# Encoder block on one core: sums of row blocks made in the merging stage and kept in DRAM, and a new start of the up-projection

## The chip, the cores and the metric

The kernel runs as one launch on one core of one Trainium2 chip. Times are device microseconds of that core, from the first to the last instruction of an execution. Its engines are TensorE (PE, with its weight loads PEld), VectorE (DVE), ScalarE (ACT), GpSimd (POOL) and SyncE (SP, which only issues DMAs).

## The reference

One encoder block over 2048 tokens of 1024 channels, in float32. What matters here is its end:

```
merged = sigmoid(g_a) * br_a + sigmoid(g_b) * br_b      # attention branch, conv branch
x  = x + merged @ w_out
h2 = rmsnorm(x, norm2_g)
up = dwconv3(h2 @ w_up)                # w_up: 1024 x 5632
gate, val = split(up, 2)
x  = x + (gelu(gate) * val) @ w_down   # w_down: 2816 x 1024
out = rmsnorm(x, norm_f_g)
```

## The kernel before

Every float32 operand of a matmul is split into a high part (ACT copies it, rounded, line 88) and a low part (DVE subtracts, line 89), and a product is three matmuls: high by high, high by low, low by high.

The program has three stages. The first makes the input projection, attention and convolution; the change leaves it alone. The second, the merging stage (`phase_b`), goes over four quads of 512 tokens. A quad has 8 blocks of `merged`, then four token tiles of 128 tokens with 48 matmuls of `w_out` each (line 835). Behind a token tile, DVE adds the residual (L844) and SP stores it; ACT sums the squares (L125), POOL works out the inverse root in eight tiny steps (L119, L105, then L108 and L109 three times) and DVE scales the rows (L850). `h2_tiles` then transposes two such tiles, chunk by chunk of 128 channels, on PE (L872); ACT copies them out times the norm's gain (L875) and SP stores them to the DRAM tensor `h2` (L877). These steps lie between matmuls of later tiles. The last two tiles have none to lie between.

The third stage is the feed-forward. Tokens are halved: `phase_up(0)`, `phase_down(0)`, `phase_up(1)`, `phase_down(1..3)`. `phase_up` multiplies by `w_up` in 22 pairs of row blocks, a gate block and a value block of 128 channels, by a form with seven products instead of eight. With A the weights (two blocks of channels by two halves of K) and B the activations (two halves of K by two blocks of 512 tokens), the products are A11·B11, A12·B21, S1·T1, S2·T2, S3·T3, S4·B22 and A22·T4. S1 to S4 are sums of weight blocks, T1 to T4 sums of activation blocks. Each product is 12 matmuls of 128x512 (four chunks `kc` of K, three each, line 951), 84 for a pair.

At the start of each `phase_up`, `h_raw` loads two blocks of 512 KB from `h2` for each `kc` (L894), POOL makes T1 to T4 out of them (L905, four of 128x512), and ACT and DVE split the seven tiles `h`. The split tiles stay, 28 of them, for all 22 pairs. `w_raws` loads two blocks of 512 KB of weights for a pair (L923), POOL makes four sums (L934 to L937), and seven tiles `w` are split. For the first pair, `head` issues three of the products `kc` by `kc`, so that they can run while the tiles arrive; from then on `unit` takes product after product.

PE's instructions stand in the order of the code, which in the merging stage interleaves transposes by a period in matmuls. The other engines' orders come from the program's builder. Each queue is in order: an instruction that waits holds those behind it. SP issues nearly all DMAs.

Of the kernel before, what the change touches and what calls it, by code (L numbers as in the profile page):

```python
# [12 lines left out]
F32 = mybir.dt.float32  # L13
# [42 lines left out]
PAD_ACT = 256  # L56
F_RAW, F_W, F_U, F_C, F_BLK = 4, 9, 3, 2, 4
# [4 lines left out]
TAGS_B = {"gt": "gt", "x": "x", "lv": "lv", "h2": "h2", "y": "y"} | {n: "l" for n in _LN}  # L62
BUFS_B = {"gt": 2, "x": 4, "l": 6, "lv": 1, "h2": 4, "y": 1}
# [14 lines left out]
class Block:  # L78
# [651 lines left out]
    def phase_b(self):  # L730
        nc, a = self.nc, self.a
        mm = nc.tensor.matmul
# [81 lines left out]
        def main():  # L814
# [5 lines left out]
            for qd in range(4):  # L820
# [6 lines left out]
                for tt in range(4):  # L827
# [23 lines left out]
                    xs.append(y)  # L851
# [4 lines left out]
                self.sides.append([self.h2_tiles(xs[2:4], t0 - 128), 2.4, -4.0])  # L856
# [6 lines left out]
    def h2_tiles(self, xs, t0):  # L863

        n = 2
        st = None
        for kc in range(KC):
            if kc % n == 0:
                st = self.T([128, n, 256], name="h2")
            ps = self.pp.tile([128, 512], F32, name="pt", tag="s")  # L870
            for i, x in enumerate(xs):
                self.nc.tensor.transpose(  # L872
                    ps[:, i * 128 : i * 128 + 128], x[:, kc * 128 : kc * 128 + 128], self.ident
                )
            self.nc.scalar.activation(st[:, kc % n], ps[:, :256], AF.Copy, scale=self.col(C_G2, kc))  # L875
            if kc % n == n - 1:
                self.nc.sync.dma_start(  # L877
                    self.h2[kc - n + 1 : kc + 1, :, t0 : t0 + 256].rearrange("k p t -> p k t"), st
                )
            yield  # L880
# [8 lines left out]
    def h_raw(self, half, kc):  # L889
        t0 = half * HALF  # L890
        out = []
        for k in (kc, kc + 4):
            r = self.k4("hraw", "raw", F_RAW)
            self.nc.sync.dma_start(r, self.h2[k, :, t0 : t0 + HALF])  # L894
            out.append(r)
        return out
# [62 lines left out]
    def phase_up(self, half):  # L959
# [41 lines left out]
        def unit(f, W, tail, u):  # L1001
# [6 lines left out]
            if tail:  # L1008
                tail()
# [208 lines left out]
```

## Time and profile before

| | us |
|---|---|
| median of 3 runs | 2851.57 (2850.73 to 2852.62) |
| the profiled execution | 2845.32 |
| its span | 2843.5 |
| PE busy | 2729.9 (96%) |
| DVE, ACT, POOL busy | 1939.1, 1184.8, 543.7 |
| mean granted TensorE clock | 0.979 |

The page cuts the span into 40 slices of 71 us. The merging stage fills slices 16 to 20, `phase_up(0)` begins in slice 21 at about 1435 us and `phase_up(1)` in slice 29 at about 2016 us. Two rows of the slices stand in the section on rows, below. Busy time of matmuls is modelled and a few per cent of matmul records can be missing, so a count (x46) may be a little low.

### The profile page before, as it was taken

The numbers are of one execution on the slowest core, as the hardware profiler recorded it, in microseconds if no ns is written. First come the engines' busy times: TensorE is split into PE (matmuls) and PEld (weight loads), VectorE is DVE, ScalarE is ACT, GpSimd is POOL, SyncE is SP. The second block draws the span as 40 slices with busy tenths as digits, with TensorE's granted clock in tenths as the row PEclk, the third lists the DMA queues.
The fourth block names the chain that finished last, engine by engine and source line by source line (L and its number), as shares of the span: only waits on it lengthen the run. The fifth ranks groups of instructions, "written<-read, shape, count | busy, mean of one in ns | idle before, by whom it ended". The sixth has DMA issues, their size and how long they took to land.

```text
span 2843.5 us, 34321 instructions
## 1 busy us (share of the span) xinstructions
PE 2729.9 (96%) x12597; PEld 2254.7 (79%) x12597; DVE 1939.1 (68%) x2636; ACT 1184.8 (42%) x1880; POOL 543.7 (19%) x698
## 2 busy tenths in 40 slices
PE   8998999999999999999959999999799999999998
PEld 6786788888888878888838888888588888888877
DVE  4697999677876746665368888883588888834342
ACT  6422222256655633332245455452354554533231
POOL 1101000000000001001054444421544344102021
PEclk9999999999999999999969999999899999999999
DMA  5357733589788777766342222254222222555451
GB/s 176 96 155 238 249 120 118 159 219 256 208 241 221 208 244 237 245 208 208 100 138 89 85 89 75 88 188 146 96 90 82 89 75 83 197 173 191 141 185 52
DMA packets 408215, 444.79 MB, mean 156 GB/s; under 512 B 25218, under 2 KB 321902, under 8 KB 407022
## 3 DMA queue, kind: packets, MB, share of 16 engines
q1 hardware_dynamic: 408045, 442.59, 50.0%
q8 instruction: 99, 1.62, 0.2%
q14 instruction: 71, 0.57, 0.1%
HBM read 325.27 MB, written 133.71 MB: 161 GB/s over the span
## 4 chain that ended last, share of the span: by engine, by line
PE 77%; issue 8%; DMA 7%; DVE 3%; POOL 3%; SPq 1%; ACT 1%; ACTq 0%; POOLq 0%; DVEq 0%
PE bank L951 29%; PE bank L1091 16%; PE mm L292 7%; PE mm L290 7%; PE mm L294 7%; PE mm L835 2%; PE ot L609 2%; PE s L564 2%; PE pt L590 2%; POOL rt L108 1%; DVE acc L439 1%; DMA qs<-qh 1%; DMA ks<-kh 1%; POOL ht L905 1%; DMA hraw<-h 1%
## 5 line engine op out<-in xcount | busy, mean ns | idle before, releaser
L951 PE MATMUL bank<-h,w 128*128 128x512 f32 x3696 | 861.4, 395 | 50.1 <-ACT h L88 35.9
L951 PEld LDWEIGHTS bank<-h,w 128*128 128x128 f32 x3696 | 702.8, 191 | 207.9 <-ACT h L88 39.6
L1091 PE MATMUL bank<-wd,g 128*128 128x512 f32 x2112 | 482.0, 390 | 7.0 <-DVE x L1104 7.0
L290 PE MATMUL mm<-act,wh 128*128 128x512 f32 x1152 | 459.9, 399 | 13.2 <-ACT qt L337 6.5
L1091 PEld LDWEIGHTS bank<-wd,g 128*128 128x128 f32 x2112 | 397.5, 188 | 90.5 <-DVE x L1104 5.9
L292 PE MATMUL mm<-act,wh 128*128 128x512 f32 x1152 | 460.8, 400 | 0.0
L294 PE MATMUL mm<-act,wl 128*128 128x512 f32 x1152 | 458.2, 398 | 0.2 <-DVE wl L89 0.2
L439 DVE SCALAR_TENSOR_TENSOR acc<-u,dw,acc 128x1008 f32<-128x1008 f32 (+1 forms) x240 | 310.9, 1296 | 5.8
L290 PEld LDWEIGHTS mm<-act,wh 128*128 128x128 f32 x1152 | 218.6, 190 | 54.1 <-ACT qt L337 7.8
L294 PEld LDWEIGHTS mm<-act,wl 128*128 128x128 f32 x1152 | 218.7, 190 | 37.1 <-DVE wl L89 0.7
L89 DVE TENSOR_TENSOR wd<-draw,wd 128x1024 fp32r<-128x1024 f32 x88 | 107.5, 1223 | 205.9 <-ACT wd L88 201.2
L292 PEld LDWEIGHTS mm<-act,wh 128*128 128x128 f32 x1152 | 218.5, 190 | 36.1 <-DVE act L245 0.3
L89 DVE TENSOR_TENSOR w<-wraw,w 128x512 fp32r<-128x512 f32 x176 | 194.0, 1119 | 36.4 <-ACT w L88 36.3
L88 ACT ACTIVATE wd<-draw 128x1024 fp32r<-128x1024 f32 x88 | 93.3, 1061 | 259.6 <-DMA draw<-in_w_down 258.8
L88 ACT ACTIVATE wh<-wraw 128x1024 fp32r<-128x1024 f32 x102 | 108.0, 1059 | 213.1 <-PE mm L292 167.7
L982 DVE SCALAR_TENSOR_TENSOR c<-u,fw,c 128x1023 f32<-128x1023 f32 (+1 forms) x88 | 139.1, 1581 | 64.3 <-ACT c L981 63.2
L89 DVE TENSOR_TENSOR wl<-wraw,wh 128x1024 fp32r<-128x1024 f32 x102 | 125.0, 1225 | 51.6 <-ACT wh L88 51.2
L88 ACT ACTIVATE w<-wraw 128x512 fp32r<-128x512 f32 x176 | 108.7, 626 | 102.0 <-PE bank L951 80.9
L119 POOL TENSOR_SCALAR v<-ms 128x1 f32<-128x1 f32 x36 | 11.7, 324 | 696.8 <-ACT mm L125 360.2
L88 ACT ACTIVATE w<-ws 128x512 fp32r<-128x512 f32 x132 | 82.5, 626 | 145.1 <-PE bank L951 127.8
L983 DVE SCALAR_TENSOR_TENSOR c<-u,fw,c 128x1023 f32<-128x1023 f32 (+1 forms) x88 | 142.5, 1620 | 0.2
L835 PE MATMUL mm<-woh,act 128*128 128x512 f32 x512 | 141.3, 393 | 0.6 <-DVE gt L802 0.6
(168 smaller groups left out, 3783.7 us busy)
## 6 DMA issues: line engine op xcount, KB each, us to landing
wraw<-in_w_up SPq DMA_DIRECT2D x88, 512.0 KB
draw<-in_w_down SPq DMA_DIRECT2D x88, 512.0 KB
wraw<-in_w_in SPq DMA_DIRECT2D x72, 512.0 KB
graw<-gd SPq DMA_DIRECT2D x44, 512.0 KB
gs<-gate SPq DMA_DIRECT2D x64, 256.0 KB
q<-qs SPq DMA_DIRECT2D x64, 256.0 KB
v<-vs SPq DMA_DIRECT2D x128, 128.0 KB
gt<-gs SPq DMA_DIRECT2D x32, 512.0 KB
```

Of the source, the lines that this page charges most:

```text
L88: self.nc.scalar.activation(hi, src, AF.Copy)
L89: self.nc.vector.tensor_tensor(lo, src, hi.bitcast(F32), op=ALU.subtract)
L290: mm(ps, wh[:, kc], X[kc][:, 0:512], start=kc == 0, stop=False)
L292: mm(ps, wh[:, kc], X[kc][:, 512:1024], start=False, stop=False)
L294: mm(ps, wl[:, kc], X[kc][:, 0:512], start=False, stop=kc == KC - 1)
L439: tap = nc.vector.scalar_tensor_tensor(acc, u[:, k : k + n], w(k), acc, ALU.mult, ALU.add)
L564: nc.tensor.matmul(ps[:, :w], q[:, s * 512 + rt * 128 : s * 512 + rt * 128 + 128], kv[:, r0 : r0 + nr, st : st + 32], start=s == 0, stop=s ...
L835: mm(ps[:, nh], l, r[kc][:, nh * 512 : nh * 512 + 512], start=kc == 0 and l is mh and r is woh, stop=kc == KC - 1 and l is ml,)
L951: self.nc.tensor.matmul(ps, w[:, x, kc], h[:, y], start=first and kc == 0 and i == 0, stop=kc == 3 and i == 2, skip_group_check=True,)
L982: nc.vector.scalar_tensor_tensor(c, u[:, 0:n], tap(0), c, ALU.mult, ALU.add)
L983: nc.vector.scalar_tensor_tensor(c, u[:, 2 : 2 + n], tap(2), c, ALU.mult, ALU.add)
L1091: mm(ps[tt][nh], x[:, tok], y[:, c], start=f == 0 and i == 0, stop=f == NF - 1 and i == 2,)
```

## The change

Merging stage. `h2_tiles` now goes over chunk pairs (`kc`, `kc+4`) and `h2_step` makes the sums there. For the first block of 512 tokens of each half it only stores B11 and B21. For the second it loads these back from DRAM (`hb`), POOL makes T1, T2, T3 and T4 (four subtractions of 128x256) and SP stores T1, T2, T3 with B22, and T4. All seven operands stay in a DRAM tensor `hc`, ready made. The last 256 tokens are not transposed in the merging stage: their scaled rows are stored to a DRAM tensor `yn`, and `h2_late` loads, transposes, sums and stores them inside `phase_up(0)`, a chunk pair behind each of the pairs 4 to 7. They belong to the second half of the tokens, which only `phase_up(1)` reads.

Feed-forward. `h_tile` loads one operand tile (256 KB) and splits it; there are no sums of activations left there. `duo` runs the pairs 0 and 1 side by side, product by product, and asks for operand tiles in the order of their use (B11, T1, T2, B21, B22, T3, T4). The weight sum S2 is made in the place of A11. `layout` sets which freed tiles of the stage before each tile of the feed-forward lies over; the 28 tiles for `h` get four tags, and `phase_down(0)` uses only two of them for its weights (12 tiles in place of 28).

```diff
-                    y, junk = x, ps.rearrange("p b t -> p (b t)")
-                    if qd == 3 and tt >= 2:
-                        y = junk = self.ap.tile([128, 1024], F32, name="act", tag="act")[:, :D]
-                    r = self.rstd(self.sumsq(x, junk), D)
-                    nc.vector.tensor_scalar(y, x, r, None, ALU.mult)
+                    r = self.rstd(self.sumsq(x, ps.rearrange("p b t -> p (b t)")), D)
+                    nc.vector.tensor_scalar(x, x, r, None, ALU.mult)
...
-                self.sides.append([self.h2_tiles(xs[2:4], t0 - 128), 2.4, -4.0])
+                    if qd == 3 and tt >= 2:
+                        nc.sync.dma_start(self.yn[tt - 2], x)
+                if qd < 3:
+                    self.sides.append([self.h2_tiles(xs[2:4], t0 - 128), 2.4, -4.0])
...
+    def h2_step(self, kc, e, t0, xs, ps, st, b0, t2):
...
+        if b0 is not None and e == 0:
+            nc.sync.dma_start(b0, two(0))
+        for i, x in enumerate(xs):
+            nc.tensor.transpose(ps[:, e * 256 + i * 128 : e * 256 + i * 128 + 128], x, self.ident)
+        nc.scalar.activation(st[:, e], ps[:, e * 256 : e * 256 + 256], AF.Copy, scale=self.col(C_G2, kc + 4 * e))
+        if e == 0:
+            return
+        if b0 is None:
+            nc.sync.dma_start(two(0), st)
+            return
+        sub = lambda o, x, y: nc.gpsimd.tensor_tensor(o, x, y, op=ALU.subtract)
+        t2 = t2[:, 0]
+        sub(b0[:, 0], st[:, 0], b0[:, 0])
+        sub(t2, st[:, 1], b0[:, 0])
+        sub(st[:, 0], st[:, 1], st[:, 0])
+        sub(b0[:, 1], b0[:, 1], t2)
+        nc.sync.dma_start(hc[H_AT["T1"], :, t], b0[:, 0])
+        nc.sync.dma_start(hc[H_AT["T2"], :, t], t2)
+        nc.sync.dma_start(two(H_AT["T3"]), st)
+        nc.sync.dma_start(hc[H_AT["T4"], :, t], b0[:, 1])
...
+    def h_tile(self, H, half, name, kc):
+        r = self.k4("hraw", "hraw", 4, (128, 512))
+        self.nc.sync.dma_start(r, self.hc[half, kc, H_AT[name]])
...
+        t = H[name, kc] = self.k4("h", shape=(128, 2, 512), dtype=F32R, **self.h_tag(j))
+        self.split(t[:, 0], t[:, 1], r)
...
+        def duo():
...
+            sums = [self.w_sums(self.w_raws(0)), None]
+            for name in ("A11", "S1"):
+                self.w_split(W[0], sums[0], name)
+            build("B11")
...
+            self.product(A[0], W[0], "A11", H, "B11", first=True)
...
+            sums[1] = self.w_sums(self.w_raws(1))
+            build("T1")
...
+            self.product(E[0], W[0], "S1", H, "T1", first=True)
...
+            for name in ("A11", "S1"):
+                self.w_split(W[1], sums[1], name)
+            build("T2")
...
+            self.product(A[1], W[1], "A11", H, "B11", first=True)
...
+            self.product(E[1], W[1], "S1", H, "T1", first=True)
...
+            both = lambda name: [self.w_split(W[i], sums[i], name) for i in range(2)]
+            both("S2")
+            build("B21")
+            for i in range(2):
+                self.product(A[i], W[i], "S2", H, "T2")
...
+            both("A12")
+            build("B22")
+            for i in range(2):
...
+                self.product(B, W[i], "A12", H, "B21", first=True)
...
+            both("S4")
+            build("T3")
+            for i in range(2):
+                self.product(E[i], W[i], "S4", H, "B22")
...
+            both("S3")
+            build("T4")
...
+            for i in range(2):
+                self.product(A[i], W[i], "S3", H, "T3")
...
+            both("A22")
+            self.product(A[0], W[0], "A22", H, "T4")
...
-                wh = self.k4("wd", "h", 28, dtype=F32R)
-                wl = self.k4("wd", "h", 28, dtype=F32R)
+                order = (2, 2, 2, 3, 3, 3) + (0, 0, 0, 0, 1, 1, 1, 1) * (g > 0)
+                wh, wl = [self.k4("wd", dtype=F32R, **self.h_tag(order[f % len(order)])) for _ in range(2)]
...
-    nc = _bacc.Bacc("TRN2", target_bir_lowering=False, num_devices=1)
+    nc = _bacc.Bacc("TRN2", target_bir_lowering=False, num_devices=1, dynamic_dma_scratch_size=1024)
```

SP's queue at the end of the merging stage, before. `h_67` is the DRAM tensor `h2`, `x_66` the residual; a number behind `h` is that of a buffer, `Activation_49` that of a semaphore of ACT.

```order
934 L845 DMA x_66<-x 128x1024 [waits DMAHW3_49,DVE_49]
935 L877 DMA h_67<-h_13254 128x2x256 [waits DMAHW4_49,Activation_49]
936 L877 DMA h_67<-h_13264 128x2x256 [waits DMAHW5_49,Activation_49]
937 L877 DMA h_67<-h_13274 128x2x256 [waits DMAHW6_49,Activation_49]
938 L877 DMA h_67<-h_13284 128x2x256 [waits DMAHW7_49,Activation_49]
939 L923 DMA wraw<-in_w_up 128x8x128 [waits DMAHW0_49]
940 L923 DMA wraw<-in_w_up 128x8x128 [waits DMAHW1_49,PE_49]
941 L894 DMA hraw<-h_67 128x1024 [waits DMAHW2_49]
942 L894 DMA hraw<-h_67 128x1024 [waits DMAHW3_49]
```

The same place now; `hb` and `hd` hold sums, `hc` and `yn` are the new DRAM tensors:

```order
979 L905 DMA hc<-hd 128x256 [waits Pool_49]
980 L906 DMA hc<-h_13304 128x2x256 [waits Activation_49,Pool_49]
981 L907 DMA hc<-hb 128x256 [waits Pool_49]
982 L907 DMA hc<-hb 128x256 [waits DMAHW4_49,Pool_49]
983 L861 DMA yn<-x 128x1024 [waits DMAHW5_49,DVE_49]
984 L945 DMA wraw<-in_w_up 128x8x128 [waits DMAHW6_49]
985 L945 DMA wraw<-in_w_up 128x8x128 [waits DMAHW7_49,PE_49]
986 L934 DMA hraw<-hc 128x512 [waits DMAHW0_49]
987 L934 DMA hraw<-hc 128x512 [waits DMAHW1_49]
988 L934 DMA hraw<-hc 128x512 [waits DMAHW2_49]
989 L934 DMA hraw<-hc 128x512 [waits DMAHW3_49]
```

The first weights stood behind the last store of `h2`, which waits for ACT; they stand now behind the store of the last scaled rows, which waits for DVE, and behind stores of sums, which wait for POOL.

POOL's queue there, before; L119, L105, L108 and L109 are the steps of the last inverse root:

```order
199 L119 TENSOR_SCALAR v<-ms 128x1 [waits Activation_49]
200 L105 TENSOR_SCALAR r<-v 128x1 [waits DVE_49,Pool_49]
201 L108 TENSOR_SCALAR rt<-r,v 128x1 [waits Pool_49]
202 L109 TENSOR_SCALAR r<-rt,r 128x1 [waits Pool_49]
203 L108 TENSOR_SCALAR rt<-r,v 128x1 [waits Pool_49]
204 L109 TENSOR_SCALAR r<-rt,r 128x1 [waits Pool_49]
205 L108 TENSOR_SCALAR rt<-r,v 128x1 [waits Pool_49]
206 L109 TENSOR_SCALAR r<-rt,r 128x1 [waits Pool_49]
207 L934 TENSOR_TENSOR ws<-wraw 128x512 [waits DMAHW0_49,DMAHW1_49,DVE_49,PE_49]
208 L935 TENSOR_TENSOR wraw<-wraw 128x512 [waits Pool_49]
209 L905 TENSOR_TENSOR ht<-hraw 128x512 [waits DMAHW2_49,DMAHW6_49,DVE_49,PE_49]
```

The same place now (L124, L110, L113 and L114 are those steps, L898 the subtractions of the sums):

```order
236 L898 TENSOR_TENSOR hb<-h_13267,hb 128x256 [waits DMAHW0_49,DMAHW2_49,Activation_49,Pool_49]
237 L124 TENSOR_SCALAR v<-ms 128x1 [waits Activation_49]
238 L898 TENSOR_TENSOR hb<-h_13304,hb 128x256 [waits DMAHW3_49,DMAHW1_49,Pool_49]
239 L898 TENSOR_TENSOR hd<-h_13267,hb 128x256 [waits Pool_49]
240 L898 TENSOR_TENSOR h_13267<-h_13267 128x256
241 L110 TENSOR_SCALAR r<-v 128x1 [waits DVE_49,Pool_49]
242 L898 TENSOR_TENSOR hd<-h_13304,hb 128x256 [waits DMAHW5_49,Pool_49]
243 L898 TENSOR_TENSOR h_13304<-h_13304 128x256 [waits DMAHW4_49]
244 L898 TENSOR_TENSOR hb<-hb,hd 128x256 [waits Pool_49]
245 L113 TENSOR_SCALAR rt<-r,v 128x1 [waits Pool_49]
246 L898 TENSOR_TENSOR hb<-hb,hd 128x256 [waits Pool_49]
247 L114 TENSOR_SCALAR r<-rt,r 128x1 [waits Pool_49]
```

Seven subtractions now stand inside the last inverse root and one just ahead of it, and the first two of these eight wait for loads from `hc`. The sums of activations (L905) that stood behind the first sums of weights are gone.

DVE's queue around the end of `phase_down(0)`, before; `x<-bank` (L1104) are the adds behind its last matmuls, `h` and `w` are splits for `phase_up(1)`:

```order
1881 L89 TENSOR_TENSOR h<-hraw,h 128x512 [waits DMAHW3_49,Activation_49]
1882 L89 TENSOR_TENSOR h<-ht,h 128x512 [waits Activation_49]
1883 L89 TENSOR_TENSOR w<-ws,w 128x512 [waits Activation_49]
1884 L89 TENSOR_TENSOR w<-wraw,w 128x512 [waits Activation_49]
1885 L89 TENSOR_TENSOR w<-ws,w 128x512 [waits Activation_49] x2
1886 L1104 TENSOR_TENSOR x<-bank,x 128x512 [waits PE_49] x8
1887 L1123 SCALAR_TENSOR_TENSOR x<-x,r,gf 128x1024 [waits Activation_49,Pool_49]
1888 L89 TENSOR_TENSOR w<-wraw,w 128x512 [waits DMAHW4_49,Activation_49]
1889 L89 TENSOR_TENSOR w<-wraw,w 128x512 [waits DMAHW5_49,Activation_49]
1890 L1123 SCALAR_TENSOR_TENSOR x<-x,r,gf 128x1024 [waits DVE_49,Pool_49] x2
1891 L89 TENSOR_TENSOR h<-ht,h 128x512 [waits Activation_49]
1892 L89 TENSOR_TENSOR h<-hraw,h 128x512 [waits Activation_49]
```

The same place now (L94 is the split, L1191 the add):

```order
1873 L94 TENSOR_TENSOR h<-hraw,h 128x512 [waits Activation_49] x2
1874 L94 TENSOR_TENSOR w<-wraw,w 128x512 [waits Activation_49]
1875 L94 TENSOR_TENSOR h<-hraw,h 128x512 [waits Activation_49] x2
1876 L1191 TENSOR_TENSOR x<-bank,x 128x512 [waits PE_49]
1877 L94 TENSOR_TENSOR w<-wraw,w 128x512 [waits Activation_49]
1878 L1191 TENSOR_TENSOR x<-bank,x 128x512 [waits PE_49]
1879 L94 TENSOR_TENSOR h<-hraw,h 128x512 [waits DMAHW4_49,Activation_49]
1880 L1191 TENSOR_TENSOR x<-bank,x 128x512 [waits PE_49] x2
1881 L94 TENSOR_TENSOR h<-hraw,h 128x512 [waits DMAHW5_49,Activation_49]
1882 L1191 TENSOR_TENSOR x<-bank,x 128x512 [waits PE_49] x2
1883 L94 TENSOR_TENSOR h<-hraw,h 128x512 [waits DMAHW7_49,Activation_49]
```

Before, four of the 28 splits of `h` for the second half stand ahead of these adds (two of them above) and 24 behind them. Now 16 stand ahead of them (B11, T1, T2 and, the last four, B21 above), and four (B22) between and just behind them.

## Rows read from the trace of the kernel before

**Rows 1.** The page, busy tenths in 40 slices of 71 us: TensorE, VectorE, granted clock.
```profile
PE   8998999999999999999959999999799999999998
...
DVE  4697999677876746665368888883588888834342
...
PEclk9999999999999999999969999999899999999999
```

**Rows 2.** Windows: length, PE and PEld of L951 (last row all engines), clock, DMA, GB/s.
```profile
1424.20:1500.30 76.10, 36.20 (x102) 23.91 (x103) 0.64 0.45 141
2015.75:2060.40 44.65, 23.74 (x63) 16.29 (x63) 0.69 0.38 132
...
1490.00:1500.00 10.00, 10.00 (x46) 8.29 (x45) 8.03 (x12) 5.82 (x10) 4.80 (x6) 1.00 0.75 207
```

**Rows 3.** Timeline of PE, 1420 to 1500 us: start, length, operation [idle before].
```profile
1423.59 0.60 PE L872 MATMUL pt<-ident,x 128*128 128x128 f32 x4
...
1430.08 0.69 PE L872 MATMUL pt<-ident,act 128*128 128x128 f32 x2 [4.81 <-DVE act L850]
...
1444.06 0.80 PE L951 MATMUL bank<-h,w 128*128 128x512 f32 x1 [9.17 <-ACT h L88]
...
1463.90 4.10 PE L951 MATMUL bank<-h,w 128*128 128x512 f32 x10 [3.37 <-DVE h L89]
...
1482.90 17.37 PE L951 MATMUL bank<-h,w 128*128 128x512 f32 x65 [3.69 <-ACT h L88]
```

**Rows 4.** The chain that ended last, 1425 to 1500 us: start, length, what.
```profile
1435.84 0.46 SPq L923
...
1436.40 5.68 DMA wraw<-in_w_up
...
1446.90 0.64 ACT h L88
...
1472.32 3.18 DMA hraw<-h
```

**Rows 5.** Timeline of DVE, 1424 to 1500 us.
```profile
1429.27 0.75 DVE L850 TENSOR_SCALAR act<-x,r 128x1024 f32<-128x1024 f32 x1 [4.26 <-POOL r L109]
1440.96 0.69 DVE L89 TENSOR_TENSOR w<-wraw,w 128x512 fp32r<-128x512 f32 x1 [10.94 <-ACT w L88]
...
1452.39 1.75 DVE L89 TENSOR_TENSOR w<-wraw,w 128x512 fp32r<-128x512 f32 x1
1454.06 1.76 DVE L89 TENSOR_TENSOR w<-ws,w 128x512 fp32r<-128x512 f32 x1
...
1457.55 0.68 DVE L89 TENSOR_TENSOR w<-ws,w 128x512 fp32r<-128x512 f32 x1
1458.15 2.36 DVE L89 TENSOR_TENSOR w<-wraw,w 128x512 fp32r<-128x512 f32 x2
```

**Rows 6.** Timeline of POOL, 1424 to 1500 us.
```profile
1426.34 0.19 POOL L119 TENSOR_SCALAR v<-ms 128x1 f32<-128x1 f32 x1 [8.97 <-ACT act L125]
...
1428.97 0.27 POOL L109 TENSOR_SCALAR r<-rt,r 128x1 f32<-128x1 f32 x1
1442.24 1.27 POOL L934 TENSOR_TENSOR ws<-wraw 128x512 f32<-128x512 f32 x1 [13.01 <-DMA wraw<-in_w_up]
...
1451.88 1.71 POOL L937 TENSOR_TENSOR ws<-wraw,ws 128x512 f32<-128x512 f32 x1
```

**Rows 7.** Timeline of PE at the start of the second up-projection, 1985 to 2064 us.
```profile
2015.78 2.65 PE L951 MATMUL bank<-h,w 128*128 128x512 f32 x11
...
2031.85 1.22 PE L951 MATMUL bank<-h,w 128*128 128x512 f32 x2 [11.89 <-ACT h L88]
```

**Rows 8.** Waits of PE, 2000 to 2062 us: waited for, us in total, times, longest.
```profile
PE bank L951 <- ACT h L88: 19.2, 3, 11.9
```

**Rows 9.** Windows, all engines: PE, PEld, DVE, ACT, POOL, then clock, DMA share, GB/s.
```profile
1990.00:2000.00 10.00, 10.00 (x46) 8.29 (x45) 0.00 (x0) 0.00 (x0) 0.00 (x0) 1.00 0.01 2
...
1170.00:1420.00 250.00, 250.00 (x1176) 207.32 (x1175) 130.43 (x205) 73.06 (x120) 24.75 (x88) 1.00 0.58 187
```

More of the change, by code (lines that the diff above doesn't have):

```diff
@@ L731, in phase_b @@
         nc, a = self.nc, self.a
+        for name, w in (("gt", 1024), ("sq", 512), ("lv", 384), ("y", 512), ("h2", 512), ("hb", 512), ("hd", 256), ("x", D)):
+            self.T([128, w], name=name)
         mm = nc.tensor.matmul
@@ L918, in w_raws, with h_tag @@
+    def h_tag(self, j):
+        return dict(tag=f"h{j}", bufs=F_H[j])
+    def h_tile(self, H, half, name, kc):
+        r = self.k4("hraw", "hraw", 4, (128, 512))
+        self.nc.sync.dma_start(r, self.hc[half, kc, H_AT[name]])
+        i = H_PLACE.index(name) * 4 + kc
+        j = next(j for j in range(4) if i < sum(F_H[: j + 1]))
+        t = H[name, kc] = self.k4("h", shape=(128, 2, 512), dtype=F32R, **self.h_tag(j))
+        self.split(t[:, 0], t[:, 1], r)
     def w_raws(self, f):
@@ L987, in phase_up @@
         blk = [slice(o + 512 * b, o + 512 * b + 512) for b in range(2)]
-        def head(f, W, kcs, u):
-            if kcs[0] == 0:
-                u.update(A=self.bank(), D=self.bank(), B=self.bank())
-            for bank, a, b in (("A", "A11", "B11"), ("D", "S1", "T1"), ("B", "A12", "B21")):
-                self.product(u[bank], W, a, H, b, kcs, True)
         def snap(ps):
@@ new lines, in gelu, with unit @@
+        def gelu(f, u):
+            gate = conv(u, f)
+            nc.scalar.activation(gate, gate, AF.Gelu)
+            return gate
+        def unit(f, W, tail):
+            A = self.bank()
+            self.product(A, W, "A11", H, "B11", first=True)
+            s1 = snap(A)
+            tail()
+            E = self.bank()
+            self.product(E, W, "S1", H, "T1", first=True)
+            s5 = snap(E)
+            self.product(A, W, "S2", H, "T2")
+            s2 = snap(A)
+            ua = u_tile(f)
+            B = self.bank()
+            self.product(B, W, "A12", H, "B21", first=True)
+            add(ua[:, blk[0]], B, s1)
+            self.product(A, W, "S3", H, "T3")
+            ub = u_tile(NF + f)
+            add(ub[:, blk[1]], A, s5)
+            self.product(E, W, "S4", H, "B22")
+            add(ua[:, blk[1]], E, s2)
+            gate = gelu(f, ua)
+            def tail():
+                self.product(A, W, "A22", H, "T4")
+                nc.scalar.activation(ub[:, blk[0]], A, AF.Copy)
+                gated(f, gate, ub)
+            return tail
@@ L1051, in phase_up @@
+        tail = duo()
+        wr = {f: self.w_raws(f) for f in (2, 3)}
+        Ws = {2: self.w_side(wr.pop(2))}
+        for f in range(2, NF):
             if f + 1 < NF:
@@ L1054, in phase_up @@
                 wr[f + 2] = self.w_raws(f + 2)
-            tail = unit(f, Ws.pop(f), tail, us[f] if f < 1 else {})
+            tail = unit(f, Ws.pop(f), tail)
+            if half == 0 and 4 <= f < 8:
+                self.h2_late(f - 4)
         tail()
@@ L1162, in run @@
         self.x2 = dt("x2", [S, D])
-        self.h2 = dt("h2", [8, 128, S])
+        self.hc = dt("hc", [2, 4, 7, 128, 512])
+        self.yn = dt("yn", [2, 128, D])
         self.gd = dt("gd", [NF, 128, S])
```

206 lines of the change are left out of this document (100 added, 106 removed).

## The prediction

> **What bounds the kernel now.** I read the page first. TensorE is 96% busy, so only the places where it is not can give anything. The 40 slices show two dips, the digits 5 and 7 of PE, and the granted clock falls in the same slices [rows 1]. Cutting both by windows and counting the matmuls of L951 gives their price. In full flow 46 matmuls take 10.00 us at a clock of 1.00, 0.217 us each [rows 2]. The first dip, from the last transposes beside matmuls (1424.2) to the point from which PE runs unbroken (1500.3), lasts 76.1 us and holds 102 matmuls, 22.2 us of work: **53.9 us are lost**. The second (2015.75 to 2060.4) lasts 44.65 us and holds 63, 13.7 us of work: **31.0 us are lost**. Both are starts of an up-projection.
>
> The timeline of PE tells what the first is made of. Sixteen transposes wait for the last scaled rows (4.8 us before the first of 1430.08), the first product waits until 1444.06 for its operands, then small groups of matmuls alternate with waits of about 3 us, and only the 65 from 1482.90 are unbroken [rows 3]. In between the clock is at its lower level of 1.2 GHz (0.64 over the window, a mean of both levels), ten matmuls taking 4.10 us after idle time [rows 2, 3]. The chain says what feeds them: SP issues the first weights at 1435.84, they land 5.68 us after 1436.40, then POOL, DVE and loads of 512 KB (3.18 us) take turns [rows 4]. The timeline of DVE gives the price of a 128x512 split: 0.68 us at a spacing of 0.60 when it is alone, 1.75 at 1.67 while POOL makes sums [rows 5]; a POOL sum of 128x512 takes 1.27 us alone and 1.71 beside DVE [rows 6]. By a rule of the Trainium skill (SBUF — State Buffer, Who interferes with whom), GpSimd and a VectorE operation with two SBUF inputs hold a shared port in turns, one blocking the other; rows 5 and 6 agree, and by the rule the new sums of the merging stage slow DVE there too, which I price below from rows.
>
> At the second dip PE waits 19.2 us for ACT's splits of `h`, 11.9 of it in one wait [rows 8], between 2019.96 and 2031.85, while DVE, ACT and POOL had done nothing from 1990 to 2000 [rows 7, 9]. The inputs were there; the work was queued behind the end of `phase_down(0)`.
>
> **The change, first start.** (a) The weights' issue. It stays behind a result of the merging stage: now the store to `yn`, which needs DVE's scaling (L850), which needs POOL's root. Before, the root took from 1426.34 to 1429.24 [rows 6], and the scaling ended at 1430.02 [rows 5]. Now eight subtractions of 128x256 stand in and ahead of it. Half of a 128x512 sum is 0.64 to 0.86 us, so 5.1 to 6.9 us: root at 1434.3, scaling until 1435.1, weights issued at about 1435.5, as before. If the subtractions are through earlier, 5 us are gained; if the load from `hc` that they wait for is late by a store and a load of 3.18, 6 us are lost. I take 0. The stores and loads of sums in SP's queue stand ahead of the same point and are in this. The 16 transposes go from here, but lay in time in which the weights were awaited: nothing gained.
>
> (b) From the weights to unbroken matmuls. Before, POOL made 4 x 4 sums of activations and eight of weights in this time, and DVE ran at the slow spacing for most of it. Now only the eight weight sums of pairs 0 and 1 are left, 8 x 1.71 = 13.7 us. DVE has 28 + 14 = 42 splits. At best 8 at 1.67 and 34 at 0.60 follow each other from 1440.96: 13.4 + 20.4, T4 ready at 1474.8. At worst all go at 1.67: 1511. Between lie the loads: four slots for tiles, so four tiles a round of issue 0.46, load at most 3.18, ACT 0.64, DVE 0.68, some 5.0 us [rows 4, 5]. With the two first rounds slowed by POOL, I get B11 at 1450, T1 at 1460, and T4 between 1485 and 1492. PE is then through 13 of 14 products, 156 matmuls, at about T4 + 0.7; unhindered it would be there at 1424.2 + 156 x 0.217 = 1458.1. The loss is 28 to 35 us, I take 31: **gain 23**. From the ends: loss 17 (gain 36) at best, and at worst all of the 53.9 (gain 0). That the loads are half as large need not make them cheaper: the Trainium skill (DMA: Bandwidth & Descriptors, Anatomy of one DMA — SWDGE (gpsimd) path) gives about 2 us of every transfer as fixed. For that reason too I leave 3.18 for the half-sized load, whose duration no row shows.
>
> **Second start.** The order puts B11, T1, T2 and B21 of the second half, and weights, ahead of the end of `phase_down(0)`, into time in which DVE was idle [rows 9]. Eight products, 96 matmuls, 20.8 us, then need nothing new; in that time DVE has 12 tiles left, three rounds of 5.0 us, and some eight weight splits, 0.68 to 1.75 each. It keeps ahead or is late by a few us: of the 31.0, 20 to 31 are won, I take **30**, since 15 + 8 x 0.68 = 20.4 just fits.
>
> **What it costs.**
> - The 16 transposes now cost PE time inside `phase_up(0)`: 0.60 us for four [rows 3], **2** for all (1 to 4).
> - 16 subtractions there, behind pairs 4 to 7: up to 0.86 x 4 = 3.4 us of a blocked DVE for each pair of 84 x 0.217 = 18.2 us. DVE is 80 to 90% busy in those slices [rows 1], so 2 to 3 us of slack remain and hide most of it. I take **2** (0 to 6).
> - 48 subtractions in the merging stage: 31 to 41 us of POOL in 250, where POOL has 25 busy and DVE 130 [rows 9]. PE is covered unless a transpose or a residual add gets late, by one DVE operation each time. I take **3** (0 to 10). If the cover goes, the third rival happens.
> - `phase_down(0)` has 12 weight tiles for 28: a load and its split come later, but 96 matmuls of a block of four last 20.8 us, and four loads and splits less. I take **1** (0 to 4).
> - Reading twice the sums instead of once the rows costs DMA traffic, at a share of 0.45 in the first start [rows 2]: nothing beyond the rounds above.
>
> Sum: 23 + 30 - 2 - 2 - 3 - 1 = 45. The profiled execution took 2845.32, so 2800.3. The median of the runs shown is 6.3 above that execution: 2806.6, rounded to **2806**.
>
> **Rivals.**
> 1. *Only the second start gains.* DVE keeps the slow spacing through the first, since POOL turns to the sums of pairs 2 and 3 and each load waits for a slot: gain 0 there. For it: every input of the first start still depends on weights issued at about 1435.5. Against: 16 of 24 sums are gone. 45 - 23 = 22: 2829.
> 2. *Both starts are nearly covered.* The first loses only the 17 us of its lower end, the second nothing, the costs other than transposes are hidden: 36 + 31 - 2 = 65: 2786. Against it: the four slots.
> 3. *Slower: the round trip through `hc` stalls PE in the merging stage.* T4 is stored to where B11 or B21 was read, and the next loads wait for that landing. PE's transposes are in order; if ACT finds no free buffer (three for copies, two for `hb`), the transpose behind it waits and with it all matmuls. A chunk pair needs a store and a load, 2 x 3.18, and four subtractions, 2.6 to 3.4, together 9 to 10 us; the code gives it two steps of 1.9 or 2.4, 3.8 to 4.8 us. If each of the 12 chunk pairs held PE for the difference, 5.2, the price would be 62 and the result 45 - 62 = -17: 2868. It decides from 45 / 12 = 3.8 us per chunk pair. Against it: two are in flight at once, and a group of four is followed by a pause of about as long. By the Trainium skill's 2 us of fixed cost (DMA: Bandwidth & Descriptors, the section named above) it would be an estimated 2 x 2.0 + 3 = 7 us at least, and less of a stall.
> 4. *The change does not do what it says at the second start*: the tiles for B11 to B21 find their slots taken, by the last readers in `phase_up(0)` or by weights of `phase_down(0)`, and wait until its end. Then the 31 stay lost: 2836.
>
> **How the numbers follow.** Chances: forecast 0.60, rival 1 0.17, rival 2 0.13, rival 3 0.05, rival 4 0.05. The forecast's own bounds (gain 0 to 36 at the first start, 20 to 31 at the second) spread wider than my belief; 2784 to 2838 takes in rivals 1, 2 and 4 and leaves out rival 3 and the ends of several terms at once. A difference under 0.2% (5.7 us) can't be told from none. Faster: all but rival 3 and a heap of costs, 0.91; same 0.04; slower 0.05.
>
> **What would show it.** In the profile after: L905 is gone from the groups of POOL, and subtractions of 128x256 stand in the merging stage. (a) is right if the first weights are issued between 1433 and 1438; (b) if DVE's spacing falls to 0.60 after about 1456, T4 is split before 1492 and unbroken matmuls begin near there. The second start is right if the windows from the end of `phase_down(0)` on show PE at 10.00 of 10 and a clock of 1.00. Rival 3 would show as waits of PE for ACT's copies before 1420, and windows of the merging stage under 20.00 of 20. The forecast is wrong if the first start still loses over 45 us, or the second over 10.

## The result, and the profile after

The changed kernel takes 2804.82 us (median of 4 runs, 2802.58 to 2805.53) against 2851.15 us (median of 4 runs before, 2844.9 to 2852.62): a ratio of 0.984, 95% interval 0.9828 to 0.9852, or 46 us less. Forecast were 2806 and a range of 2784 to 2838. The two profiled executions are nearer to each other: 2845.32 and 2805.53, spans 2843.5 and 2803.7, 39.8 us. The profiled execution of before lies 5.8 us under its kernel's median, and the account below, made between the two traces, has 39.8 us to explain, not 46.

The page after, PE and granted clock in the 40 slices (before: [rows 1]):

```profile
PE   7998999999999999999969999999999999999998
...
PEclk9999999999999999999989999999999999999999
```

One dip is left, in slice 21; that of the second start has gone. To compare like with like I cut 80 us from the last matmul of the merging stage (DVE's last residual add starts within half a microsecond of it), and 50 us at the start of `phase_up(1)`, and count only matmuls of the up-projection. Columns: start:end, length, PE (count), PEld (count), clock, DMA share, GB/s. Before:

```profile
1424.20:1504.20 80.00, 40.10 (x120) 27.11 (x121) 0.66 0.43 135
2015.78:2065.78 50.00, 29.12 (x87) 20.73 (x87) 0.73 0.45 147
```

After:

```profile
1439.20:1519.20 80.00, 54.49 (x215) 42.37 (x216) 0.83 0.70 219
2018.70:2068.70 50.00, 50.00 (x222) 41.42 (x221) 1.00 0.45 144
```

The last window begins 3.5 us behind the first matmul of `phase_up(1)`, which comes at 2015.22; from there 221 stand in 50 us. It is unbroken flow, 222 records in 50 us, 0.2252 us each with the records that are missing. By that measure 80 us hold 355. The first start lost 235 x 0.2252 = 52.9 us before and loses 31.5 after. The second lost 135 x 0.2252 = 30.4 and loses nothing.

The first start also begins 15.0 us later, at 1439.2 for 1424.2. Of this, 3.2 us are there already at the first matmul of the merging stage (1042.9 for 1039.7), before any of the new work; it starts between 1040.5 and 1045.6 in the runs e1 to e12, and no run shows why. Most of the rest arises between the last residual adds of the second and the third quad. DVE's timeline, before:

```profile
1237.06 1.23 DVE L844 TENSOR_TENSOR x<-mm,x 128x1024 f32<-128x1024 f32 x1 [0.51 <-PE mm L835]
...
1332.76 1.23 DVE L844 TENSOR_TENSOR x<-mm,x 128x1024 f32<-128x1024 f32 x1 [5.05 <-PE mm L835]
```

and after:

```profile
1239.97 1.22 DVE L851 TENSOR_TENSOR x<-mm,x 128x1024 f32<-128x1024 f32 x1
...
1348.00 1.23 DVE L851 TENSOR_TENSOR x<-mm,x 128x1024 f32<-128x1024 f32 x1 [4.87 <-PE mm L842]
```

95.7 us lie between them before and 108.0 after: 12.3 us, in one quad. Windows in it show PE short of work (columns as in [rows 9]). In the first two DVE and POOL are both at work; in the third POOL is idle and the DMA engines are busy 0.99 of the time:

```profile
1250.00:1260.00 10.00, 8.89 (x43) 6.91 (x41) 5.73 (x11) 1.90 (x3) 5.04 (x12) 1.00 0.91 294
1260.00:1270.00 10.00, 7.42 (x35) 5.72 (x34) 9.90 (x16) 3.40 (x6) 4.34 (x6) 1.00 0.59 184
1290.00:1300.00 10.00, 7.36 (x32) 5.74 (x31) 5.92 (x10) 2.83 (x4) 0.21 (x1) 0.95 0.99 293
```

What PE waits for there is mostly split weights and gates (1090 to 1440 us: in total, times, longest):

```profile
PE mm L806 <- DVE wl L94: 3.1, 4, 1.9
PE mm L842 <- DVE gt L809: 2.6, 1, 2.6
```

SP issues the loads of both (L773, L781) in one queue with the stores of sums (L907) and the loads back (L889):

```profile
1251.76 0.32 SPq L907 DMA_DIRECT2D hc<-hb  x1
1252.17 0.40 SPq L773 DMA_DIRECT2D wraw<-in_w_na_out  x1
...
1253.28 1.50 SPq L889 DMA_DIRECT2D hb<-hc  x2
1255.48 0.36 SPq L781 DMA_DIRECT2D gt<-gs  x1
```

At the end of the stage, POOL does what the order said. Its timeline after: the first line waits for a load from `hc`, the steps of the last root stand between subtractions, and the first weights wait for both.

```profile
1441.87 0.72 POOL L898 TENSOR_TENSOR hb<-h,hb 128x256 f32<-128x256 f32 x1 [4.67 <-DMA hb<-hc]
1442.69 0.19 POOL L124 TENSOR_SCALAR v<-ms 128x1 f32<-128x1 f32 x1
...
1449.89 0.27 POOL L114 TENSOR_SCALAR r<-rt,r 128x1 f32<-128x1 f32 x1
```

SP's queue there:

```profile
1450.97 0.32 SPq L861 DMA_DIRECT2D yn<-x  x1
1451.34 1.50 SPq L945 DMA_DIRECT2D wraw<-in_w_up  x2
```

The root takes 7.5 us in place of 2.9 [rows 6], and the weights go out at 1451.34, 12.2 us behind the last matmul; before it was 11.6 (1435.84 and 1424.2 [rows 4]). PE then has nothing for 19.8 us (timeline of PE after):

```profile
1459.25 3.88 PE L985 MATMUL bank<-h,w 128*128 128x512 f32 x7 [19.80 <-ACT h L93]
1463.35 0.97 PE L985 MATMUL bank<-h,w 128*128 128x512 f32 x3 [0.22 <-DVE h L94]
1466.71 1.22 PE L985 MATMUL bank<-h,w 128*128 128x512 f32 x2 [2.39 <-DVE h L94]
1469.14 12.31 PE L985 MATMUL bank<-h,w 128*128 128x512 f32 x45 [1.21 <-ACT h L93]
1482.83 0.51 PE L985 MATMUL bank<-h,w 128*128 128x512 f32 x1 [1.38 <-ACT h L93]
1483.56 16.62 PE L985 MATMUL bank<-h,w 128*128 128x512 f32 x72 [0.22 <-DVE h L94]
```

Where [rows 3] have groups of one to ten matmuls with waits of about 3 us, this has long runs, and from 1483.56 on PE is not held. The last of the 28 splits of `h`, a tile of T4, comes much later (timeline of DVE; below it the window from 1483.56 to its end, columns as in the windows of the first start):

```profile
1509.85 0.68 DVE L94 TENSOR_TENSOR h<-hraw,h 128x512 fp32r<-128x512 f32 x1
```

```profile
1483.56:1510.53 26.97, 26.97 (x119) 22.34 (x120) 1.00 0.74 234
```

A third place had not been in the forecast. The timeline of PE of before, between the last two down-projections:

```profile
2706.10 0.93 PE L1091 MATMUL bank<-wd,g 128*128 128x512 f32 x3 [1.53 <-DVE x L1104]
2712.47 2.08 PE L1091 MATMUL bank<-wd,g 128*128 128x512 f32 x4 [5.43 <-DVE x L1104]
```

PE needs banks that DVE's adds have not emptied, 7.0 us in all. After, the trace lists no wait of PE from 2015 us to the end.

The account, between the traces (last matmul of the merging stage, start of `phase_up(1)`, end): 1424.2, 2015.78, 2843.5 before; 1439.2, 2015.22, 2803.7 after.

| stretch | forecast | measured |
|---|---|---|
| up to the end of the merging stage (3.2 of it ahead of the stage) | -3 | -15.0 |
| first start (52.9 - 31.5) | +23 | +21.4 |
| rest of `phase_up(0)` and `phase_down(0)` | -5 | -5.8 |
| second start | +30 | +30.4 |
| rest, the waits between down-projections in it | 0 | +8.8 |
| sum | 45 | 39.8 |

### The profile page after: what moved, and what is told of

It reads as the page before. It is cut to its first block, busy times and chain, and to the rows that moved or that the text cites. A ratio compares the mean times of both kernels' runs of the same rounds, so it can differ in the third digit from the quotient of the medians.

```text
span 2803.7 us, 34637 instructions
## 1 busy us (share of the span) xinstructions
PE 2715.3 (97%) x12597; PEld 2247.2 (80%) x12597; DVE 1886.3 (67%) x2636; ACT 1185.6 (42%) x1880; POOL 555.4 (20%) x731
## 3 DMA queue, kind: packets, MB, share of 16 engines
q1 hardware_dynamic: 427533, 461.47, 52.9%
## 4 chain that ended last, share of the span: by engine, by line
PE 75%; DMA 9%; issue 6%; DVE 5%; POOL 2%; ACT 2%; SPq 1%; ACTq 0%; POOLq 0%; DVEq 0%
PE bank L985 26%; PE bank L1178 17%; PE mm L297 7%; PE mm L295 7%; PE mm L299 7%; PE ot L614 2%; PE s L569 2%; PE pt L595 2%; PE mm L842 1%; DMA bd<-rext 1%; DMA gt<-gs 1%; SPq L216 1%; DMA hraw<-hc 1%; DMA y<-ys 1%; PE mm L802 1%
## 5 line engine op out<-in xcount | busy, mean ns | idle before, releaser
L985 PE MATMUL bank<-h,w 128*128 128x512 f32 x3696 | 847.0, 391 | 26.2 <-ACT h L93 22.4
L985 PEld LDWEIGHTS bank<-h,w 128*128 128x128 f32 x3696 | 695.1, 188 | 174.1 <-ACT h L93 23.8
L94 DVE TENSOR_TENSOR w<-wraw,w 128x512 fp32r<-128x512 f32 x220 | 206.9, 953 | 106.5 <-ACT w L93 106.2
L94 DVE TENSOR_TENSOR wd<-draw,wd 128x1024 fp32r<-128x1024 f32 x88 | 107.0, 1222 | 177.0 <-ACT wd L93 176.5
L93 ACT ACTIVATE w<-wraw 128x512 fp32r<-128x512 f32 x220 | 135.9, 626 | 164.7 <-PE bank L985 132.6
L1016 DVE SCALAR_TENSOR_TENSOR c<-u,fw,c 128x1023 f32<-128x1023 f32 (+1 forms) x88 | 131.7, 1496 | 62.1 <-ACT c L1015 61.6
L94 DVE TENSOR_TENSOR wl<-wraw,wh 128x1024 fp32r<-128x1024 f32 x102 | 126.5, 1241 | 51.9 <-ACT wh L93 47.3
L1015 ACT ACTIVATE c<-u,cols,fw 128x1023 f32<-128x1023 f32 (+1 forms) x88 | 109.5, 1245 | 64.7 <-DVE c L1030 37.0
L124 POOL TENSOR_SCALAR v<-ms 128x1 f32<-128x1 f32 x36 | 10.5, 291 | 628.7 <-ACT junk L130 314.6
```

The source lines that it names most:

```text
L93: self.nc.scalar.activation(hi, src, AF.Copy)
L94: self.nc.vector.tensor_tensor(lo, src, hi.bitcast(F32), op=ALU.subtract)
L985: self.nc.tensor.matmul(ps, w[:, x, kc], h[:, y], start=first and kc == 0 and i == 0, stop=kc == 3 and i == 2, skip_group_check=True,)
L1015: nc.scalar.activation(c, u[:, 1 : 1 + n], AF.Identity, scale=tap(1), bias=self.col(C_FFB, ch))
L1016: nc.vector.scalar_tensor_tensor(c, u[:, 0:n], tap(0), c, ALU.mult, ALU.add)
```

## The experiments

Each ratio is to the kernel before on the same chip; d is the distance of the two adds above (95.7 before, 108.0 after), and "first loss" is what the first 80 us lose, counted as above.

**e1: no subtractions in the merging stage.**

```diff
+        if t0 == S - 256:
             sub(b0[:, 0], st[:, 0], b0[:, 0])
...
+        else:
+            t2 = st[:, 1]
```

> The changed kernel without the 48 subtractions of the merging stage; what was loaded and copied is stored in place of the sums, so T1 to T4 of most tokens are not computed. Loads, stores and SP's queue stay as they are. In the changed kernel the last residual add of the second quad comes at 1239.97 us and that of the third at 1348.00, 11.9 us later than before the change (95.7 us apart in place). Theory A (VectorE is held up by GpSimd's subtractions in the blocks of the third quad): most of the 12 us goes, the two adds stand 97 us or less apart, PE idles under 2 us between 1245 and 1320. Theory B (SP's queue is held by the round trip through hc): the distance stays at 105 us or more, since loads and stores are all there. Theory C (DMA bandwidth): the same as B. In any theory the last inverse root has nothing between its steps, so the first weights are issued about 7 us behind the last matmul of the merging stage in place of 12.2: 5 us gained. Whole time: A 2788, B and C 2799.

Measured: 2789.87, ratio 0.9791 (0.9769 to 0.9813). d is 95.7, all of its delay gone, though the quad before it takes 100.1 us for 96.3 in the changed kernel (table under e9). The weights are issued 7.0 us behind the last matmul. So the subtractions are needed for the delay of d. A and what later was called D (below) are left; B, as put here, and C fall, since all loads and stores were there.

**e2: no loads back.**

```diff
-        if b0 is not None and e == 0:
+        if b0 is not None and e == 0 and t0 == S - 256:
             nc.sync.dma_start(b0, two(0))
...
+        back = (b0[:, 0], b0[:, 1]) if t0 == S - 256 else (st[:, 1], st[:, 0])
-        sub(b0[:, 0], st[:, 0], b0[:, 0])
+        sub(b0[:, 0], st[:, 0], back[0])
```

> The changed kernel without the loads of B11 and B21 back into the merging stage; the subtractions take other operands of the same size from the copies at hand, so T1 to T4 of most tokens are wrong. All 48 subtractions and all stores stay. Theory A (VectorE held up by the subtractions): the adds that end the second and third quad stay about 107 us apart, the time about 2803. Theory B (SP and POOL held by the round trip): the distance falls to 98 or less, time about 2793. Theory C (DMA bandwidth): a part of it, the loads are 3 of 12 MB moved there, so 1 to 3 us. The last inverse root no longer waits for a load, so up to 5 us may come at the first start in each theory.

Measured: 2792.21, ratio 0.9801 (0.978 to 0.9823), d 100.4. Neither 107 nor 98: with all subtractions in place most of the delay goes, which A alone cannot explain, but 4.7 us of it stay.

**e3: the second group of a quad spread out.**

```diff
-                    self.sides.append([self.h2_tiles(xs[2:4], t0 - 128), 2.4, -4.0])
+                    self.sides.append([self.h2_tiles(xs[2:4], t0 - 128), 6.0, -4.0])
```

> The changed kernel with the transposes and subtractions of the second pair of tiles of a quad spread over more matmuls: a step each 6.0 us in place of 2.4, so eight steps over 48 us of the next quad's blocks. Theory A (VectorE beside a burst of subtractions): the distance of the two adds falls from 108 us to about 100, time about 2797. Theory B (round trip): each chunk pair now has 12 us for a round trip of 9 to 10, so SP is not held either: about the same 2797. If neither holds but DMA bandwidth, no change: 2805.

Measured: 2799.79, ratio 0.9827 (0.9805 to 0.9849), d 100.4, as both theories forecast for d, so it does not tell A from B.

**e4: the last stores on ACT's queue.**

```diff
+        q = nc.scalar if t0 == S - 512 else nc.sync
-        nc.sync.dma_start(hc[H_AT["T1"], :, t], b0[:, 0])
+        q.dma_start(hc[H_AT["T1"], :, t], b0[:, 0])
...
-                        nc.sync.dma_start(self.yn[tt - 2], x)
+                        nc.scalar.dma_start(self.yn[tt - 2], x)
```

> The changed kernel with the stores of the last group of sums and of the last scaled rows issued from ACT's queue in place of SP's. Theory (the first weights wait only for their place in SP's queue): they are issued at about 1441 in place of 1451, right behind the last residual rows, PE's wait of 19.8 us ahead of the first product falls to about 10, time about 2795. Rival: ACT is held in its own queue by stores that wait for subtractions until 1447, the first split of A11 starts no sooner than that, and POOL's sums of weights queue behind the same subtractions until 1450: PE's wait falls by no more than 4 us, time 2801 or more.

Measured: 2800.72, ratio 0.9828 (0.9806 to 0.9851). The weights were issued at 1445.56, 6.7 us behind the last matmul, but PE's first wait fell only to 15.4: ACT's store of the scaled rows stood until 1451.2 ahead of its first split (1451.29). This is nearer the rival: the queue was one gate, the root another.

**e5: the subtractions aside.**

```diff
+            for _ in range(4):
+                sub(t2, st[:, 0], st[:, 1])
+            t2 = st[:, 1]
```

> The changed kernel in which the 48 subtractions of the merging stage stay, with the same size and engine, but work on copies at hand into a tile that nobody stores; loads and stores stay and carry other data (T1 to T4 of most tokens are wrong). So SP's stores, and the weights and gates queued behind them, wait for no subtraction, and no subtraction for a load. Without subtractions the last adds of the second and third quad stood 95.7 us apart, without loads 100.4, in the changed kernel 108.0. Theory A (VectorE shares time with GpSimd's subtractions): the distance stays at 102 or more. Theory D (SP's queue is held by stores that wait for subtractions that wait for loads, and the weights and gates of the quad come late): 97 or less. Whole time: A 2800, D 2790.

Measured: 2798.46, ratio 0.9818 (0.9799 to 0.9836), d 98.8, between the two marks and nearer to D. But d flatters this run: the quad before takes 102.2 us, where the changed kernel has 96.3, and both quads together take 201.1, within the 200.5 to 204.3 of the runs that keep all the waits (table under e9). The edit makes a delay of its own, so e5 does not show what 48 subtractions cost beside VectorE; e9 to e11 tell more.

**e6: the starts kc by kc, as before, with ready sums.**

```diff
-        tail = duo()
+            for kc in range(4):
+                for name in ("B11", "T1", "B21", "T2", "T3", "B22", "T4"):
+                    self.h_tile(H, half, name, kc)
+                for ps, x, y in ((A, "A11", "B11"), (E, "S1", "T1"), (B, "A12", "B21")):
+                    self.product(ps, W, x, H, y, (kc,), True)
```

> The changed kernel with the start of each up-projection as it was before: pair 0 alone, all seven sums of a chunk kc loaded, three products kc by kc, then pair 1; the sums still come ready made from DRAM, and the layout stays. Theory (the order of products matters at the first start, since 28 tiles and only 36 matmuls come before the last chunk): the stretch from the last matmul of the merging stage to unbroken matmuls loses some 43 us in place of 32.8, and at the second start the first chunk waits for B21, whose slots phase_down(0) holds, so about 20 of the 31 us won there are lost again: about 2834. Rival (only the ready sums matter): less than 8 us slower, 2812 or less.

Measured: 2822.27, ratio 0.9902 (0.9885 to 0.9918), 18 us slower than the changed kernel. Its two stretches:

```profile
1435.00:1515.00 80.00, 42.15 (x134) 31.04 (x135) 0.68 0.65 197
2025.36:2075.36 50.00, 45.44 (x188) 36.12 (x188) 0.97 0.44 137
```

At the first start 221 x 0.2252 = 49.8 us are lost, nearly the 52.9 of before: there **the order is the gain** (products and loads, with two pairs side by side), and ready sums alone give 3 us. Of the 18.3 us that the old order costs, 3.5 are the first product's wait, 23.3 for 19.8. At the second start 7.7 are lost, for 30.4 before: what e6 keeps, the ready sums and the layout, suffices for most of the gain, and the order adds 7.7. The theory held for the first start and not for the second, where 20 had been expected.

**e7: phase_down(0) over all slots.**

```diff
-                order = (2, 2, 2, 3, 3, 3) + (0, 0, 0, 0, 1, 1, 1, 1) * (g > 0)
+                order = (2, 2, 2, 3, 3, 3) + (0, 0, 0, 0, 1, 1, 1, 1)
```

> The changed kernel with phase_down(0) using all 28 tiles of h for its weights, as the later ones do. Theory (the second start is won by slots that phase_down(0) leaves alone, so that B11, T1 and T2 are split before it ends): PE waits again at the second start, 15 to 30 us, time 2820 to 2834. Rival (the ready sums and the order of products win it, slots or no slots): PE's waits there stay under 5 us, time within 5 us of 2803.

Measured: 2810.88, ratio 0.9861 (0.9846 to 0.9875): some 6 us slower than the changed kernel, between what the two expected; PE's waits at the second start are 2.6 us, as the rival had it. There 202 matmuls stand in 50 us, 4.5 us lost. So the slots kept free are worth little as long as the rest stays. What e6 and e7 leave of the second start's gain, over 20 us, points to what both of them keep, sums that POOL has not to make there. The chain of before shows POOL's sums behind the steps of the last inverse root of `phase_down(0)`, and a load behind them:

```profile
2025.89 0.34 POOL rt L108
2026.23 2.45 POOL ht L905 x2
...
2029.90 4.54 DMA hraw<-h
```

ACT's first split of `h` behind the end of `phase_down(0)` waited for these sums (timeline of ACT of before):

```profile
2027.49 0.63 ACT L88 ACTIVATE h<-ht 128x512 fp32r<-128x512 f32 x1 [9.49 <-POOL ht L905]
```

Ready sums alone were not run. Nor does any run but the kernel before lack the order and the free slots together, so it stays possible that either of them makes up for the other.

**e8: a version meant to be better**, with e3's spread, e4's stores and

```diff
-                    r = self.rstd(self.sumsq(x, ps.rearrange("p b t -> p (b t)")), D)
+                    r = self.rstd(self.sumsq(x, ps.rearrange("p b t -> p (b t)")), D, nc.vector if qd == 3 and tt >= 2 else None)
...
-                        self.sides.append([self.h2_tiles(xs[0:2], t0 - 128), 1.9, -4.0])
+                        self.sides.append([self.h2_tiles(xs[0:2], t0 - 128), 1.9 if qd < 3 else 1.0, -4.0])
```

> A version that is to be better, with the whole result computed: the spread of e3, the last two inverse roots of the merging stage on VectorE in place of GpSimd, the last group's transposes at 1.0 us a step in place of 1.9, and its stores of sums on ACT's queue, so that SP has nothing ahead of the first weights but the scaled rows. Theory (the weights wait for GpSimd's subtractions by way of the root): they are issued 5 to 7 us behind the last matmul of the merging stage in place of 12.2, PE's wait ahead of the first product falls from 19.8 to about 13, and with the 5 us of e3 the time is about 2791. Rival (the first product waits for ACT, which is held by stores, or for POOL, whose subtractions still stand ahead of the sums of weights): the wait stays above 17 us, time about 2798.

Measured: 2792.28, ratio 0.9795 (0.978 to 0.9809). Weights 6.0 us behind the last matmul, PE's first wait 15.4, d 98.6: the forecast time, with a wait 2.4 longer than forecast.

**e9: four buffers for the loads back.**

```diff
-..."h2": 3, "hb": 2, "hd": 2, "y": 1}
+..."h2": 3, "hb": 4, "hd": 2, "y": 1}
```

> The changed kernel with four buffers hb for the sums loaded back in place of two, nothing else: the four loads of a group no longer wait for the group's first T4 stores to land. Theory D (subtractions wait for loads that wait for stores, and SP's queue with the weights and gates waits behind them): the last adds of the second and third quad come to 97 to 100 us apart in place of 104 to 108, the last subtractions no longer hold the last inverse root by a load (GpSimd waits under 1 us for hb at 1440), so the weights are issued some 9 us behind the last matmul in place of 12.2; time about 2794. Theory A (only VectorE's sharing with the subtractions counts): no change, 2802 or more.

Measured: 2791.92, ratio 0.9796 (0.9777 to 0.9815); the changed kernel beside it (e12) 2805.48. d 99.4, weights 9.1 us behind the last matmul (1437.78). POOL's waits for the loads back, 1200 to 1450 us, in e12 and with four buffers:

```profile
POOL hb L898 <- DMA hb<-hc: 29.4, 5, 15.2
```

```profile
POOL hb L898 <- DMA hb<-hc: 4.6, 1, 4.6
```

One number changed, every byte and subtraction the same: 25 us of POOL's waits and 13.6 us of the time go. This settles the cause of most of the delay: a load back waited until the stores out of the same buffer, two chunks earlier, had landed.

The quads in the runs, in us between the last residual adds:

| | first to second quad | second to third (d) | both |
|---|---|---|---|
| before | 97.4 | 95.7 | 193.1 |
| changed kernel, e12 | 96.3, 96.3 | 108.0, 107.5 | 204.3, 203.8 |
| e4, e6, e7 (the same in these quads) | 96.2, 96.0, 95.8 | 107.3, 104.4, 104.9 | 203.5, 200.5, 200.8 |
| e1, no subtractions | 100.1 | 95.7 | 195.9 |
| e5, subtractions aside | 102.2 | 98.8 | 201.1 |
| e9, e10, e11, four buffers | 96.2, 96.2, 96.0 | 99.4, 96.2, 96.0 | 195.6, 192.4, 191.9 |

The runs e9 to e11 keep all 48 subtractions and come within 2.5 us of before, less than the scatter of some 4 us between runs with the same quads. So what the subtractions cost beside VectorE is small here, and theory A, which wanted 2802 or more, falls.

**e10 and e11: e8 with e9's buffers**, in e10 with the last rows stored from ACT as well.

```diff
-                        nc.sync.dma_start(self.yn[tt - 2], x)
+                        (nc.scalar if tt == 3 else nc.sync).dma_start(self.yn[tt - 2], x)
```

> e8 with the four buffers of e9 and the last scaled rows stored from ACT's queue, so that SP has only the residual rows ahead of the first weights; the whole result is computed. Theory (the weights' place in SP's queue sets the first product): weights issued 2 to 3 us behind the last matmul of the merging stage in place of 6, first product about 3 us earlier than in e8, merging stage 2 to 3 us shorter: 2787. Rival (DMA completions that the weights' issue waits for, or ACT held by its stores): no better than e8, 2792 or more.

> e10 with the last scaled rows back on SP's queue, so e8 with four load buffers alone. Expected between e8 and e10: 2789; if the store from ACT in e10 holds ACT's first split, this one is the faster of the two.

Measured: 2781.83, ratio 0.9757 (0.9742 to 0.9773), and 2782.72, 0.9761 (0.9744 to 0.9777): the same, and both faster than the kernel before and the changed one. SP's queue in e10 (its last matmul of the merging stage ends at 1427.0):

```profile
1430.89 1.12 SPq L946 DMA_DIRECT2D wraw<-in_w_up  x2
1432.14 6.09 SPq L935 DMA_DIRECT2D hraw<-hc  x4
```

The weights go out 3.9 us behind, PE's first wait is 13.4 (13.8 in e11), the first loss 22.6 us, and d 96.2: the merging stage's delay is gone. Both came out better than their forecasts, e11 by 6 us; that ACT's store would matter was not seen.

**e12: the changed kernel again.**

> The changed kernel itself beside the others of this call: about 46 us under the kernel before, as measured; its distance of the adds of the second and third quad anywhere in 104 to 108, which is what the runs that left the merging stage alone showed.

Measured: 2805.48, ratio 0.9844 (0.9822 to 0.9866), d 107.5. e6 and e7 have 104.4 and 104.9, so d is good to some 2 us either way.

## Why the prediction was right or wrong

- *Second start* (forecast 30): right in size, 30.4. The trace shows what was named, PE at 10.00 of 10 and a clock of 1.00 throughout. Its reason is half shown: splits set ahead of the end of `phase_down(0)` were put first, but e7 shows that without the free slots only 4.5 us are lost, and e6 that product by product is worth 7.7. The larger part is, as far as e6 and e7 tell, POOL out of the chain; no run isolates it.
- *First start, (b)* (forecast 23, loss 28 to 35): right in size, 21.4 and 31.5, and e6 shows that the order brings most of it. DVE's splits took 1.75 us while POOL made the weight sums and 0.68 at a spacing of 0.60 behind them, as forecast. But the forecast took the loss from the time at which T4 is split, and T4 did not set it. T4 was through at 1510.5, 71.3 us behind the last matmul of the stage, where 61 to 68 were forecast; by the forecast's own sum that is a loss of 38. By then PE has 177 matmuls behind it in the trace, more than the 156 at which the sum had it. All of the loss lies ahead of 1483.56 (58 matmuls in 44.4 us), in the wait for the first product, which comes 20 us behind the last matmul as before, and in the splits of B11, T1 and T2. So the size was in part luck. Nor was the added DMA traffic worth nothing: the DMA share went from 0.43 to 0.70 there, and loads of the chain took up to 5.84 us, where 3.18 were taken.
- *First start, (a)* (forecast: as before): right against the end of the stage, 12.2 for 11.6. The clock time forecast with it, 1433 to 1438, was wrong, 1451.34, because the stage ended later.
- *Merging stage* (forecast 3, bounds 0 to 10): **the step that failed**; it cost some 12 of the 15.0. "PE is covered unless a transpose or a residual add gets late" went by busy time, of POOL 25 and of DVE 130 of 250 us. What counted was waiting in order: subtractions wait for loads that wait for landed stores (POOL waits 29.4 us so in e12), SP's stores wait for subtractions, and behind them in SP's queue wait the weights and gates of the next blocks. That is the round trip of rival 3, at one group of three and for 12 us in place of 62, but not by the path it named: PE waits 1.1 us for a transpose's rows there and none for ACT's copies of them, while it waits for weights and gates. e9 takes away only the wait of a load for its buffer and gets back 8 of the 12 of d (5 to 9 with the scatter of d); e1 takes the subtractions and gets all of them. The chain of waits after has the price of one round trip, a store out of a buffer and then the load into it, less than the 2 x 3.18 taken:

```profile
1436.53 2.52 DMA hc<-hb
1439.07 2.64 DMA hb<-hc
```

- *Price of a shared port.* The rule of the Trainium skill for VectorE and GpSimd (SBUF — State Buffer, Who interferes with whom) would put the delay on contention. The durations agree with it (a split 0.68 alone and 1.75 beside POOL, a sum 1.27 and 1.71), but the runs do not put the delay there: e9 to e11 keep every subtraction and come within 2.5 us of before over the two quads. Waiting in order made most of it.
- *Late transposes, subtractions and 12 tiles* (forecast 5 together): 5.8, with one wait for the loads from `yn` of 2.5 us, which was not in the sum.
- *Missed*: the 7.0 us between the last down-projections. They stood in the page before, in the group of L1091. After, PE waits for none of DVE's adds. Which part of the change brought that was not tried; PE has no wait there in any of the twelve runs, with all slots used (e7) or not.
- *The number.* 45 forecast and 39.8 between the traces: -12 at the merging stage and +9 at the third place nearly cancel. The median then moved by 46, since the profiled execution of before lay 5.8 us under its median and that of after 0.7 over. So 2806 against 2804.82 is closer than the steps deserve.

## What to carry to other kernels

A dip of the bound engine at the start of a stage has a chain of its own, and two starts that look alike can be freed by different things: here the order of products and loads at one, and at the other, as far as two runs tell, sums taken out of the chain. Moving work into a stage with idle engines cost here by what it made wait in order, not by its busy time: look at what each queue holds behind the new wait, and give a round trip through DRAM as many buffers as it has steps in flight. Read every wait of the bound engine in the page, small ones too, before pricing a change.

## What the runs showed that was not expected

- Loads of 256 KB were no quicker than those of 512 KB before (3.18 [rows 4]). But the DMA engines were 62 to 72% busy beside these, and 18 to 31% in 1465 to 1490 us of before, so the size is not told apart from the traffic, and no run shows how much of a load is fixed. Three of the chain of waits after:

```profile
1476.84 5.29 DMA hraw<-hc
...
1485.83 2.73 DMA hraw<-hc
...
1489.20 5.84 DMA hraw<-hc
```

- The granted clock was 0.62 over 1440 to 1450, a mean of both levels, in which PE ran nothing, and 0.50 at 1450 to 1460, the lower level of 1.2 GHz: the first seven matmuls after the 19.8 us took 3.88 us, 0.55 each with small waits, and the 45 from 1469.14 on 12.31, 0.27 each, for 0.2252 in flow. The long wait of PE cost a second time in the matmuls behind it.
- Subtractions of 128x256 took 0.74 us in the merging stage (median), within the 0.64 to 0.86 forecast, but 1.18 inside `phase_up(0)`, where DVE's slices show the digits 8 and 7.
